# A two-layer decoder trunk on one core: where the split weights begin in their tiles, and where four rows of vectors are loaded

## The chip, the cores and the metric

The kernel runs on one core of a Trainium2 chip. The core has a matrix engine (TensorE, PE in the profile; its weight loads have a row of their own, PEld), a vector engine (VectorE, DVE), a scalar engine (ScalarE, ACT), GpSimd (POOL) and SyncE (SP), which issues most transfers. The metric is the device time of one execution in microseconds (us). Before the change it is 1217.22 us, the median of three runs (1217.1 to 1217.29).

## The reference

Two layers over 512 tokens of width 1024, float32 throughout. Layer 0 mixes with sliding-window attention and a short gated convolution, layer 1 with gated linear attention (GLA). Each is followed by a gated MLP with a width-3 causal convolution between its two projections, and by a gated per-layer embedding.

```python
def _conv_ffn(h, w_up, conv_w, conv_b, w_down):
    u = _causal_depthwise_conv(h @ w_up, conv_w) + conv_b
    gate, up = jnp.split(u, 2, axis=-1)
    return (jax.nn.gelu(gate, approximate=False) * up) @ w_down

def reference(x, p, positions, mix_norm, ffn_norm, ffn_w_up, ffn_conv_w, ...):
    cos, sin = _rope_tables(positions)
    for i in range(DEPTH):
        j = i // 2
        h = _rms_norm(x, mix_norm[i])
        if i % 2 == 0:
            x = x + _attn_conv_mixer(h, cos, sin, hy_w_in[j], ..., hy_sinks[j], hy_conv_w[j], hy_w_out[j])
        else:
            x = x + _gla_mixer(h, gla_w_in[j], gla_w_gate_up[j], ..., gla_w_out[j])
        x = x + _conv_ffn(_rms_norm(x, ffn_norm[i]), ffn_w_up[i], ffn_conv_w[i], ffn_conv_b[i], ffn_w_down[i])
        x = x + _per_layer_embedding(x, p[i], ple_norm[i], ple_w_gate[i], ple_w_proj[i])
    return x
```

The widths that matter: `D_MODEL` 1024, `D_FF` 2816 (so `w_up` is 1024 x 5632 and `w_down` 2816 x 1024), 8 query heads of 64 with blocks of 128 queries.

## The kernel before

**Products.** Features lie on the partitions and the 512 tokens along the free dimension. Every large product is made of float32 operands that are split in two: a high part, which ScalarE writes by copying to float32r, and a low part, the remainder, which VectorE writes. A product of two split operands is three matmuls into one PSUM bank, high by high, high by low and low by high. `mm3` (L153 to L159) issues them for the plain products; its rows in the profile are L157, L158 and L159. The weight is the stationary operand, 128 rows by 128 columns, and 512 tokens stream past it. In the value columns of the GLA mixer (`Values`, L1509) it is the other way round: the normed input is stationary, and 336 or 368 columns of a weight stream.

**Block products.** A part of the MLP's two projections is not done plainly. `seven` (L850) computes a two by two block of weights against a two by two block of activations with seven block products in place of eight. Its inner function `product` has four steps of three matmuls (L865, L866, L867), each of them 256 tokens wide. One call of `seven` is 7 x 4 x 3 = 84 matmuls. It is called for each of the 11 column groups of the up projection in both layers, four times in the first down projection and three times in the second, 29 calls in all. Its weights come in four tiles: `plain`, `t13` and `last` are split into the tiles `wh` and `wl` (by `cut_blocks` at L804 with `wide`, or by `first_forms` at L824), and `t2`, which serves one of the seven block products, into two smaller tiles of the pool `sp`.

**Tiles.** `wh` and `wl` are tags of the pool `wp`: three buffers each, 1024 elements of four bytes per partition, one behind the other. Ahead of them in the pool stand two buffers `raw` of 8,192 bytes, into which the weights are loaded. Each of the six tiles of 4,096 bytes begins at a multiple of 512 bytes of its partition, and every stationary block of 128 columns is 512 bytes of it. The normed inputs (tags `a0`, `a1`, `b0`, `b1`) and the forms for the block products (tag `four`) begin at multiples of 256 bytes. In `Values` a step of the weight is 336 or 368 elements, 1,344 or 1,472 bytes, so that the streamed operand of every second step begins 64 bytes behind a multiple of 128. The plain products split their weights with `cut` (L118). Behind `wp` lie the pools `sp` and `sm` and those of the stages, the last of which ends 696 bytes short of the partition's 229,376 bytes.

**Order.** TensorE runs in the order in which the kernel writes its matmuls (`manual_schedule`); on the other engines the framework's scheduler chooses. In layer 0's mixer `behind(n)` hangs work behind the n-th of 96 steps of the input projection (`conv_in`, eight contraction steps for each of 12 outputs). Behind step 88 (`probs_at[3]`) stand the mixture of block 2, the transposes of block 3's probabilities (`probs`, L625, rows L633, L639, L641) and then `load_vectors_ffn(0)`; behind step 93 (`mix_at`) stands the mixture of values for block 3 (`mix`, L643, row L650). `load_vectors_ffn` takes the MLP's convolution weights and biases in two calls of `columns` (L198): transfers from GpSimd's queue into a tile `vrow` (two buffers), one transpose on TensorE (L216), one copy by ScalarE (L217). The same function is called again for layer 1.

**Around it.** In an up projection one turn of the loop over groups is 84 matmuls of 256 columns, 48 of 512 columns for the value columns (`value`, L940), and the convolution taps on VectorE (`taps`, L913, rows L919 and L925), whose input is the tile `z` with a row of 514 elements, of which 512 are used.

Of the kernel before, what the change touches and what calls it, by code (L numbers as in the profile page):

```python
# [9 lines left out]
F32 = mybir.dt.float32  # L10
# [4 lines left out]
ALU = mybir.AluOpType  # L15
# [41 lines left out]
class Kernel:  # L57
# [51 lines left out]
    def weights(self, src, na, nb, by="b"):  # L109
        raw = self.raw(na, nb)  # L110
        self.nc.sync.dma_start(raw, src)
        return self.cut(raw, by)

    def raw(self, na, nb):
        t = self.wp.tile([P, 2048], F32, tag="raw", name=self.nm("raw"), bufs=2)
        return t[:, : na * nb].rearrange("p (a b) -> p a b", b=nb)

    def cut(self, rv, by, pool=None, bufs=3):  # L118


        nc = self.nc
        pool = pool or self.wp
        na, nb = rv.shape[1:]
        parts = []
        n = 2 if na * nb > 1024 else 1
        for k in range(n):
            if by == "b":
                a, b = na, nb // n
                v = rv[:, :, k * b : (k + 1) * b]
            else:  # L130
                a, b = na // n, nb
                v = rv[:, k * a : (k + 1) * a, :]
            h = pool.tile([P, 1024], F32R, tag="wh", name=self.nm("wh"), bufs=bufs)
            l = pool.tile([P, 1024], F32R, tag="wl", name=self.nm("wl"), bufs=bufs)
            hv = h[:, : a * b].rearrange("p (a b) -> p a b", b=b)
            lv = l[:, : a * b].rearrange("p (a b) -> p a b", b=b)
            nc.scalar.activation(hv, v, AF.Copy)  # L137
            nc.vector.tensor_tensor(lv, v, hv.bitcast(F32), ALU.subtract)  # L138
            parts.append((hv, lv))

        def get(i, c0, c1):
            if by == "b":
                b = nb // n
                k = c0 // b
                h, l = parts[k]
                return h[:, i, c0 - k * b : c1 - k * b], l[:, i, c0 - k * b : c1 - k * b]
            a = na // n
            h, l = parts[i // a]
            return h[:, i % a, c0:c1], l[:, i % a, c0:c1]

        return get
# [268 lines left out]
    def mixer0(self):  # L420
        nc, a, tc = self.nc, self.a, self.tc
        with tc.tile_pool(name="m0", bufs=1) as mp:
# [65 lines left out]
            sink = self.sm.tile([P, 16], F32, name="sink", bufs=1)[:, :NQ]  # L488
            self.late(sink[:, :1])
            nc.gpsimd.dma_start(sink, a["hy_sinks"][0:1, :].partition_broadcast(P))  # L490
            nsink = self.sm.tile([P, 16], F32, name="nsink", bufs=1)[:, :NQ]
            nc.vector.tensor_scalar_mul(nsink, sink, -1.0)
            h = HD // 2

            def normed(x, tab):
# [76 lines left out]
            def scores(t):  # L572

                w = 2 * P if t else P
                k0 = (t - 1) * P if t else 0
                mask = self.amask if t else self.amask[:, P:]
                s = ss[t] = mp.tile([P, NQ, 2 * P], F32, tag="s", name=self.nm("s"), bufs=2)
                mx, nm, den, es = (self.few(8, g) for g in ("mx", "nm", "den", "es"))
                banks = []
                for h2 in range(2):  # L580

                    pbs = [self.pa(), self.pa()]
                    banks.append(pbs)
                    for hh in range(2):
                        hq = 2 * h2 + hh
                        for g in range(2):
                            nc.tensor.matmul(
                                pbs[g][:, hh * 256 : hh * 256 + w],
                                qTs[t][64 * g : 64 * g + 64, hq, :],
                                kT[64 * g : 64 * g + 64, k0 : k0 + w],  # L590
                                start=True, stop=True,
                            )
                for h2, pbs in enumerate(banks):
                    heads = [(g, hh, 4 * g + 2 * h2 + hh) for hh in range(2) for g in range(2)]
                    for g, hh, head in heads:
                        nc.vector.tensor_tensor_reduce(
                            s[:, head, :w], pbs[g][:, hh * 256 : hh * 256 + w], mask,
                            scale=1.0, scalar=-1e30, op0=ALU.add, op1=ALU.max,
                            accum_out=mx[:, head : head + 1],
                        )  # L600

                    nc.vector.scalar_tensor_tensor(
                        out=of(nm, h2), in0=of(mx, h2), scalar=-(HD**-0.5), in1=of(nsink, h2), op0=ALU.mult,
                        op1=ALU.min,
                    )
                    nc.vector.tensor_tensor(of(es, h2), of(nm, h2), of(nsink, h2), ALU.subtract)
                    nc.scalar.activation(of(es, h2), of(es, h2), AF.Exp)
                    for g, hh, head in heads:
                        nc.scalar.activation(
                            s[:, head, :w], s[:, head, :w], AF.Exp, bias=nm[:, head : head + 1], scale=HD**-0.5,  # L610
                            accum_out=den[:, head : head + 1],
                        )
                    nc.vector.tensor_tensor(of(den, h2), of(den, h2), of(es, h2), ALU.add)
                    nc.vector.reciprocal(of(den, h2), of(den, h2))
                    h = 4 + 2 * h2
                    nc.vector.tensor_tensor(
                        s[:, h : h + 2, :w], s[:, h : h + 2, :w],
                        den[:, h : h + 2].unsqueeze(2).to_broadcast([P, 2, w]), ALU.mult,
                    )
                    for head in (2 * h2, 2 * h2 + 1):  # L620
                        nc.scalar.activation(s[:, head, :w], s[:, head, :w], AF.Copy, scale=den[:, head : head + 1])
# [122 lines left out]
                        query_turned(t + 2, qn[t + 2], self.ps)  # L744
                    probs(t)

            behind(probs_at[3])(lambda: self.load_vectors_ffn(0))
            behind(mix_at)(lambda: mix(3))
            behind(96)(lambda: conv_out(1))
            with tc.manual_schedule(engines={ET.PE}):  # L750
                R = self.spread()
# [52 lines left out]
    def cut_blocks(self, src, wide=True):  # L804

        nc = self.nc
        if wide:
            h, l = (self.wp.tile([P, 1024], F32R, tag=g, name=self.nm(g), bufs=3) for g in ("wh", "wl"))
        else:
            h, l = (self.sp.tile([P, S], F32R, tag="sq", name=self.nm("t2"), bufs=2) for _ in range(2))  # L810
        h, l = (x.rearrange("p (j n) -> p j n", n=src.shape[2]) for x in (h, l))
        nc.scalar.activation(h, src, AF.Copy)  # L812
        nc.vector.tensor_tensor(l, src, h.bitcast(F32), ALU.subtract)  # L813
        h, l = (x.rearrange("p j n -> p (j n)").rearrange("p (k n) -> p k n", n=P) for x in (h, l))
        n = 2 if wide else 1
        return lambda j, c: (h[:, n * j + c, :], l[:, n * j + c, :])
# [7 lines left out]
    def first_forms(self, ev, od, raw=None):  # L824

        nc = self.nc
        b11, b12, b21, b22 = ev[:, :, :P], ev[:, :, P:], od[:, :, :P], od[:, :, P:]
        if raw is not None:
            plain = self.cut_blocks(raw[:, :, :P])
        else:  # L830
            h, l = (self.wp.tile([P, 1024], F32R, tag=g, name=self.nm(g), bufs=3) for g in ("wh", "wl"))
            h, l = (x.rearrange("p (j u n) -> p j u n", u=2, n=P) for x in (h, l))
            for u, b in enumerate((b11, b21)):
                self.split((h[:, :, u], l[:, :, u]), b)
            plain = lambda j, c: (h[:, j, c], l[:, j, c])
        nc.vector.tensor_tensor(b11, b12, b11, ALU.subtract)
        nc.vector.tensor_tensor(b12, b22, b12, ALU.subtract)  # L837
        return plain
# [57 lines left out]
    def ffn(self, i, project, next_gain):  # L896
# [8 lines left out]
        with tc.tile_pool(name=f"ffn{i}", bufs=1) as fp:  # L905
# [5 lines left out]
                return fp.tile([P, 2, S], F32, tag="zt", name=self.nm("zt"), bufs=2)  # L911

            def taps(y, ps, f, more=None):  # L913
                z = fp.tile([P, S + 2], F32, tag="z", name=self.nm("z"), bufs=3)[:, :S]
                if more is None:
                    nc.vector.tensor_tensor(z, ps, R, ALU.mult)
                else:
# [398 lines left out]
    def ple1(self, fp):  # L1316
# [16 lines left out]

        def chunk(src):
            if count[0] % 6 < 3:
                h, l = (self.wp.tile([P, 2, H], F32R, tag=g, name=self.nm(g), bufs=3) for g in ("wh", "wl"))
            else:
                four = self.four(fp)
                h, l = four[:, :2], four[:, 2:]
            count[0] += 1  # L1340
            nc.scalar.activation(h, src, AF.Copy)
            nc.vector.tensor_tensor(l, src, h.bitcast(F32), ALU.subtract)
            return h, l
# [41 lines left out]
            return pj  # L1385

        def result():
            return fp.tile([P, S + 2], F32, tag="z", name=self.nm("so"), bufs=3)[:, :S]

        def keep(banks, tag):  # L1390
            out = []
# [33 lines left out]
        with tc.manual_schedule(engines={ET.PE, ET.DVE, ET.Activation}):  # L1425
# [30 lines left out]
            w22 = chunks(b22)  # L1456
            minus(b11, b21, b11)
            wt4 = [chunk(b11[:, :2, :])]
            nc.scalar.activation(self.few(NT, "rlo"), self.r, AF.Sigmoid)
            add(X, "s3", wt3)  # L1460
            ss = [summed(X[t], kd[t]) for t in (0, 1)]
            for t in (0, 1):
# [504 lines left out]
```

## Time and profile before

| | us |
|---|---|
| median of three runs | 1217.22 |
| the profiled execution's own time | 1216.55 |
| its span, first to last instruction | 1214.8 |
| TensorE with a matmul under way | 1207.6 |
| VectorE busy | 971.0 |
| ScalarE busy | 667.6 |
| GpSimd busy | 45.1 |

The views read are the page (busy time, the chain that ended last), the timeline (start in us, duration in us, engine, line, operation, tiles out and in, shapes, and in brackets the idle time before), the instructions of one line (durations in ns: least, median, largest) and busy time by stretches. The end of a matmul in the profile is modelled and matmuls overlap, so the pace of TensorE is read from starts: the time from one start to a later one over the number of matmuls between.

In time, the up projection of layer 0 runs from about 183 to 445 us and its down projection to 510; the same stages of layer 1 run from about 809 to 1070 and to 1117 us.

### The profile page before, as it was taken

The page shows a single profiled execution, that of the slowest core. Times are in us where ns is not written, and L with a number is a line of the kernel's source. Part 1 is how long each engine was busy: PE and PEld are TensorE (multiplying, and loading weights), DVE is VectorE, ACT ScalarE, POOL GpSimd, SP SyncE. Part 2 cuts the span into 40 slices and gives each one's busy share as a digit, 9 for nine tenths or more (in the row PEclk, how much of TensorE's full clock was granted, in tenths as well). Part 3 has the DMA queues.
Part 4 walks back from the last instruction along what each step waited for, and adds up shares of the span by engine and source line. Part 5 has one row for each costly group of instructions (what it writes and reads, how often), then busy time and mean ns, then how long its engine had stood idle before and what let it go on. Part 6 is the DMA issues. An engine that isn't in the chain of part 4 may idle for free.

```text
span 1214.8 us, 17728 instructions
## 1 busy us (share of the span) xinstructions
PE 1207.6 (99%) x7018; PEld 1049.2 (86%) x7018; DVE 971.0 (80%) x1543; ACT 667.6 (55%) x1093; POOL 45.1 (4%) x64
## 2 busy tenths in 40 slices
PE   9999999999999999999999999999999999999998
PEld 8887789999998889888988988889999999888887
DVE  6786687899998986746679876778999898978595
ACT  7466465656555644534563554555565555645374
POOL 2600000000000000000100000000000000000000
PEclk9999999999999999999999999999999999999999
DMA  7222222424242332222322222322232423322601
GB/s 220 83 93 70 73 70 76 133 70 139 70 129 79 108 120 94 95 97 85 114 93 69 73 68 70 105 83 92 81 128 70 139 70 129 123 87 96 208 1 70
DMA packets 111127, 117.61 MB, mean 97 GB/s; under 512 B 2840, under 2 KB 106322, under 8 KB 111044
## 3 DMA queue, kind: packets, MB, share of 16 engines
q1 hardware_dynamic: 109680, 115.35, 29.0%
q8 instruction: 55, 0.90, 0.3%
q0 software_dynamic: 560, 0.42, 0.3%
q10 hardware_dynamic: 804, 0.70, 0.2%
q14 instruction: 28, 0.23, 0.1%
HBM read 114.37 MB, written 2.10 MB: 96 GB/s over the span
## 4 chain that ended last, share of the span: by engine, by line
PE 92%; DVE 4%; ACT 2%; issue 0%; DMA 0%; ACTq 0%; POOL 0%; DVEq 0%
PE ps L157 13%; PE ps L158 13%; PE ps L159 13%; PE pa L158 7%; PE pa L157 7%; PE pa L159 7%; PE ps L865 6%; PE ps L867 6%; PE ps L866 6%; PE pa L867 2%; PE pa L866 2%; PE pa L865 2%; PE ps L1364 1%; PE ps L1362 1%; PE ps L1363 1%; DVE wl L138 1%
## 5 line engine op out<-in xcount | busy, mean ns | idle before, releaser
L137 ACT ACTIVATE wh<-raw 128x1024 fp32r<-128x1024 f32 (+4 forms) x154 | 152.5, 992 | 154.6 <-PE ps L158 103.2
L138 DVE TENSOR_TENSOR wl<-raw,wh 128x1024 fp32r<-128x1024 f32 (+4 forms) x154 | 175.4, 1140 | 59.2 <-ACT wh L137 58.6
L812 ACT ACTIVATE wh<-raw 128x1024 fp32r<-128x1024 f32 x78 | 82.6, 1059 | 127.8 <-DVE raw L837 65.6
L925 DVE SCALAR_TENSOR_TENSOR zt<-z,vfa,zt 128x510 f32<-128x510 f32 (+1 forms) x176 | 130.9, 746 | 11.9 <-ACT zt L923 11.2
L813 DVE TENSOR_TENSOR wl<-raw,wh 128x1024 fp32r<-128x1024 f32 x78 | 95.4, 1223 | 19.8 <-ACT wh L812 19.7
L923 ACT ACTIVATE zt<-z,vfb 128x512 f32<-128x512 f32 x88 | 71.0, 809 | 21.3 <-DVE four L976 12.8
L157 PE MATMUL ps<-b,wh 128*128 128x512 f32 x192 | 76.6, 399 | 0.0
L158 PE MATMUL ps<-b,wh 128*128 128x512 f32 x192 | 75.1, 391 | 0.0
L159 PE MATMUL ps<-b,wl 128*128 128x512 f32 x192 | 75.0, 391 | 0.0
L157 PE MATMUL pa<-a,wh 128*128 128x512 f32 x176 | 69.0, 392 | 0.0
L157 PE MATMUL pa<-b,wh 128*128 128x512 f32 x176 | 69.0, 392 | 0.0
L158 PE MATMUL pa<-a,wh 128*128 128x512 f32 x176 | 69.0, 392 | 0.0
L158 PE MATMUL pa<-b,wh 128*128 128x512 f32 x176 | 69.0, 392 | 0.0
L159 PE MATMUL pa<-a,wl 128*128 128x512 f32 x176 | 68.5, 389 | 0.0
L159 PE MATMUL pa<-b,wl 128*128 128x512 f32 x176 | 68.5, 389 | 0.0
L865 PE MATMUL ps<-four,wh 128*128 128x256 f32 x232 | 65.8, 283 | 0.0
L867 PE MATMUL ps<-four,wl 128*128 128x256 f32 x232 | 65.6, 283 | 0.0
L866 PE MATMUL ps<-four,wh 128*128 128x256 f32 x232 | 65.6, 283 | 0.0
L157 PE MATMUL ps<-a,wh 128*128 128x512 f32 x160 | 63.6, 398 | 0.0
L158 PE MATMUL ps<-a,wh 128*128 128x512 f32 x160 | 62.4, 390 | 0.0
L159 PE MATMUL ps<-a,wl 128*128 128x512 f32 x160 | 62.4, 390 | 0.0
L157 PE MATMUL ps<-uh,wh 128*128 128x512 f32 x128 | 50.3, 393 | 0.0
(472 smaller groups left out, 3517.4 us busy)
## 6 DMA issues: line engine op xcount, KB each, us to landing
raw<-in_ffn_w_up_dram SPq DMA_DIRECT2D x44, 1024.0 KB, 5.0
raw<-in_ffn_w_down_dram SPq DMA_DIRECT2D x13, 1024.0 KB, 4.7
raw<-in_hy_w_in_dram SPq DMA_DIRECT2D x8, 1024.0 KB, 5.0
raw<-in_gla_w_in_dram SPq DMA_DIRECT2D x8, 1024.0 KB, 5.1
raw<-in_ffn_w_down_dram SPq DMA_DIRECT2D x8, 768.0 KB, 4.1
raw<-in_ple_w_gate_dram SPq DMA_DIRECT2D x6, 1024.0 KB, 4.7
raw<-in_hy_w_out_dram SPq DMA_DIRECT2D x16, 256.0 KB, 4.4
raw<-in_gla_w_out_dram SPq DMA_DIRECT2D x4, 1024.0 KB, 4.7
```

Source lines behind the costliest of these rows:

```text
L137: nc.scalar.activation(hv, v, AF.Copy)
L138: nc.vector.tensor_tensor(lv, v, hv.bitcast(F32), ALU.subtract)
L157: mm(out, lh, rh, start=start, stop=False, **kw)
L158: mm(out, lh, rl, start=False, stop=False, **kw)
L159: mm(out, ll, rh, start=False, stop=stop, **kw)
L812: nc.scalar.activation(h, src, AF.Copy)
L813: nc.vector.tensor_tensor(l, src, h.bitcast(F32), ALU.subtract)
L865: mm(out, wh, xh, start=first and j == 0, stop=False, **kw)
L866: mm(out, wh, xl, start=False, stop=False, **kw)
L867: mm(out, wl, xh, start=False, stop=j == ND // 2 - 1, **kw)
L923: nc.scalar.activation(y, z, AF.Identity, scale=w2[:, f : f + 1], bias=bb[:, f : f + 1])
L925: nc.vector.scalar_tensor_tensor(out=y[:, tap:], in0=z[:, : S - tap], scalar=w[:, f : f + 1], in1=y[:, tap:], op0=ALU.mult, op1=ALU.add,)
```

## The change

The tiles `wh` and `wl` become 1056 elements long and come from one function, `weight_tiles(off)`. `cut`, and the weights of the last stage (`chunk`), take them from the tile's start; the weights of the block products (`plain`, `t13`, `last`) take 1024 elements from element 16 on, 64 bytes into the tile. The six tiles now lie 4,224 bytes apart, so they begin at 0, 128 and 256 bytes past a multiple of 512 for `wh` and at 384, 0 and 128 for `wl`; the pools behind move by 768 bytes or less. To make room, `z` and the results of the last stage lose their two spare elements, the negated sinks are written over the sinks, and the sigmoid that brings in its table writes to a tag that exists. `load_vectors_ffn(0)` is hung behind step 93, after the last mixture of values, in place of step 88. No instruction is added or removed.

```diff
--- before.py
+++ after.py
@@ -111,15 +111,20 @@
         self.nc.sync.dma_start(raw, src)
         return self.cut(raw, by)
 
+    def weight_tiles(self, off=0):
+
+        return [
+            self.wp.tile([P, 1024 + 32], F32R, tag=g, name=self.nm(g), bufs=3)[:, off : off + 1024] for g in ("wh", "wl")
+        ]
+
     def raw(self, na, nb):
         t = self.wp.tile([P, 2048], F32, tag="raw", name=self.nm("raw"), bufs=2)
         return t[:, : na * nb].rearrange("p (a b) -> p a b", b=nb)
 
-    def cut(self, rv, by, pool=None, bufs=3):
+    def cut(self, rv, by):
 
 
         nc = self.nc
-        pool = pool or self.wp
         na, nb = rv.shape[1:]
         parts = []
         n = 2 if na * nb > 1024 else 1
@@ -130,8 +135,7 @@
             else:
                 a, b = na // n, nb
                 v = rv[:, k * a : (k + 1) * a, :]
-            h = pool.tile([P, 1024], F32R, tag="wh", name=self.nm("wh"), bufs=bufs)
-            l = pool.tile([P, 1024], F32R, tag="wl", name=self.nm("wl"), bufs=bufs)
+            h, l = self.weight_tiles()
             hv = h[:, : a * b].rearrange("p (a b) -> p a b", b=b)
             lv = l[:, : a * b].rearrange("p (a b) -> p a b", b=b)
             nc.scalar.activation(hv, v, AF.Copy)
@@ -488,8 +492,7 @@
             sink = self.sm.tile([P, 16], F32, name="sink", bufs=1)[:, :NQ]
             self.late(sink[:, :1])
             nc.gpsimd.dma_start(sink, a["hy_sinks"][0:1, :].partition_broadcast(P))
-            nsink = self.sm.tile([P, 16], F32, name="nsink", bufs=1)[:, :NQ]
-            nc.vector.tensor_scalar_mul(nsink, sink, -1.0)
+            nc.vector.tensor_scalar_mul(sink, sink, -1.0)
             h = HD // 2
 
             def normed(x, tab):
@@ -600,10 +603,10 @@
                         )
 
                     nc.vector.scalar_tensor_tensor(
-                        out=of(nm, h2), in0=of(mx, h2), scalar=-(HD**-0.5), in1=of(nsink, h2), op0=ALU.mult,
+                        out=of(nm, h2), in0=of(mx, h2), scalar=-(HD**-0.5), in1=of(sink, h2), op0=ALU.mult,
                         op1=ALU.min,
                     )
-                    nc.vector.tensor_tensor(of(es, h2), of(nm, h2), of(nsink, h2), ALU.subtract)
+                    nc.vector.tensor_tensor(of(es, h2), of(nm, h2), of(sink, h2), ALU.subtract)
                     nc.scalar.activation(of(es, h2), of(es, h2), AF.Exp)
                     for g, hh, head in heads:
                         nc.scalar.activation(
@@ -744,8 +747,8 @@
                         query_turned(t + 2, qn[t + 2], self.ps)
                     probs(t)
 
-            behind(probs_at[3])(lambda: self.load_vectors_ffn(0))
             behind(mix_at)(lambda: mix(3))
+            behind(mix_at)(lambda: self.load_vectors_ffn(0))
             behind(96)(lambda: conv_out(1))
             with tc.manual_schedule(engines={ET.PE}):
                 R = self.spread()
@@ -805,7 +808,7 @@
 
         nc = self.nc
         if wide:
-            h, l = (self.wp.tile([P, 1024], F32R, tag=g, name=self.nm(g), bufs=3) for g in ("wh", "wl"))
+            h, l = self.weight_tiles(16)
         else:
             h, l = (self.sp.tile([P, S], F32R, tag="sq", name=self.nm("t2"), bufs=2) for _ in range(2))
         h, l = (x.rearrange("p (j n) -> p j n", n=src.shape[2]) for x in (h, l))
@@ -828,7 +831,7 @@
         if raw is not None:
             plain = self.cut_blocks(raw[:, :, :P])
         else:
-            h, l = (self.wp.tile([P, 1024], F32R, tag=g, name=self.nm(g), bufs=3) for g in ("wh", "wl"))
+            h, l = self.weight_tiles(16)
             h, l = (x.rearrange("p (j u n) -> p j u n", u=2, n=P) for x in (h, l))
             for u, b in enumerate((b11, b21)):
                 self.split((h[:, :, u], l[:, :, u]), b)
@@ -911,7 +914,7 @@
                 return fp.tile([P, 2, S], F32, tag="zt", name=self.nm("zt"), bufs=2)
 
             def taps(y, ps, f, more=None):
-                z = fp.tile([P, S + 2], F32, tag="z", name=self.nm("z"), bufs=3)[:, :S]
+                z = fp.tile([P, S], F32, tag="z", name=self.nm("z"), bufs=3)
                 if more is None:
                     nc.vector.tensor_tensor(z, ps, R, ALU.mult)
                 else:
@@ -1333,7 +1336,7 @@
 
         def chunk(src):
             if count[0] % 6 < 3:
-                h, l = (self.wp.tile([P, 2, H], F32R, tag=g, name=self.nm(g), bufs=3) for g in ("wh", "wl"))
+                h, l = (x.rearrange("p (a b) -> p a b", b=H) for x in self.weight_tiles())
             else:
                 four = self.four(fp)
                 h, l = four[:, :2], four[:, 2:]
@@ -1385,7 +1388,7 @@
             return pj
 
         def result():
-            return fp.tile([P, S + 2], F32, tag="z", name=self.nm("so"), bufs=3)[:, :S]
+            return fp.tile([P, S], F32, tag="z", name=self.nm("so"), bufs=3)
 
         def keep(banks, tag):
             out = []
@@ -1456,7 +1459,7 @@
             w22 = chunks(b22)
             minus(b11, b21, b11)
             wt4 = [chunk(b11[:, :2, :])]
-            nc.scalar.activation(self.few(NT, "rlo"), self.r, AF.Sigmoid)
+            nc.scalar.activation(self.few(NT, "rs", 4), self.r, AF.Sigmoid)
             add(X, "s3", wt3)
             ss = [summed(X[t], kd[t]) for t in (0, 1)]
             for t in (0, 1):
```

The order on TensorE changes in one place: the two transposes L216 stand behind the eight matmuls of the last mixture, 15 plain matmuls later than before. ScalarE's two copies L217 move with them, two splits of the mixture's result (L101) later.

## Prediction, made before the change was run

> **What bounds the kernel now.** First the page: who is busy, and whose work ends last.
>
> ```profile
> span 1214.8 us, 17728 instructions
> PE 1207.6 (99%) x7018; PEld 1049.2 (86%) x7018; DVE 971.0 (80%) x1543; ACT 667.6 (55%) x1093; POOL 45.1 (4%) x64
> PE 92%; DVE 4%; ACT 2%; issue 0%; DMA 0%; ACTq 0%; POOL 0%; DVEq 0%
> core 0: 1214.8 us, clock 1.000
> ```
>
> TensorE has a matmul under way for 99% of the span, and 92% of the chain that ended last is its own work, at the full granted clock. A change can therefore only save where it shortens the step from one matmul to the next, or one of the few waits between. So the second view is the timeline of TensorE, read from starts: a block product of 256 columns, then plain matmuls of 512.
>
> ```profile
> 183.37 0.28 PE L865 MATMUL pa<-a,wh 128*128 128x256 f32 x1
> 183.72 0.28 PE L865 MATMUL pa<-a,wh 128*128 128x256 f32 x1
> ...
> 184.80 0.40 PE L157 MATMUL pa<-a,wh 128*128 128x512 f32 x1
> ...
> 191.89 0.39 PE L157 MATMUL pa<-a,wh 128*128 128x512 f32 x1
> ...
> 192.57 0.39 PE L157 MATMUL pa<-a,wh 128*128 128x512 f32 x1
> ```
>
> From 183.72 to 184.80 lie nine matmuls of 256 columns: 0.120 us each. From 191.89 to 192.57 lie three of 512: 0.227. Twice the columns cost 0.107 more, so a column costs 0.107 / 256 = 0.417 ns, and the rest is 0.120 - 0.107 = 13.3 ns in both, the time of 32 columns. This rest, paid with each new weight, is all that an address could change. The first three from 183.37 to 183.72 took 0.35, not 0.36: one of them paid less.
>
> **The offset.** How many matmuls load a weight that now begins 64 bytes into its tile: line L865, a third of them, by weight tile.
>
> ```profile
> L865 PE MATMUL ps<-four,wh x232: 277/283/364, 193.6 to 1116.9; 128*128 128x256 f32 x116
> L865 PE MATMUL ps<-a,wh x120: 277/283/387, 187.6 to 505.6; 128*128 128x256 f32 x120
> L865 PE MATMUL pa<-four,wh x116: 277/283/287, 186.2 to 1104.1; 128*128 128x256 f32 x116
> L865 PE MATMUL ps<-b,wh x112: 277/283/387, 813.4 to 1115.5; 128*128 128x256 f32 x112
> L865 PE MATMUL ps<-four,t x88: 283/283/283, 189.1 to 1027.1; 128*128 128x256 f32 x88
> L865 PE MATMUL pa<-a,wh x60: 277/283/283, 183.4 to 497.1; 128*128 128x256 f32 x60
> L865 PE MATMUL pa<-b,wh x56: 277/283/283, 809.1 to 1106.9; 128*128 128x256 f32 x56
> ```
>
> With `wh`: 232 + 120 + 116 + 112 + 60 + 56 = 696, and as many on L866 and L867: 2088 matmuls, 2088 x 0.120 = 250.6 us of the span. The `t` rows (88 here, 28 more in smaller groups) are not touched. Each ns of step is worth 2.09 us.
>
> No row of before has a stationary weight of these products off a multiple of 128 bytes, so the cost is bounded from both sides. The nearest rows for phase are those of the GLA values, where the stream (not the weight) begins 64 bytes off in every second step of k, four token blocks, twelve matmuls, long.
>
> ```profile
> 589.56 0.33 PE L157 MATMUL ps<-wh,b 128*128 128x368 f32 x1
> ...
> 591.56 0.33 PE L157 MATMUL ps<-wh,b 128*128 128x368 f32 x1
> ...
> 593.59 0.33 PE L157 MATMUL ps<-wh,b 128*128 128x368 f32 x1
> ...
> 657.70 0.32 PE L157 MATMUL ps<-wh,b 128*128 128x336 f32 x1
> ...
> 659.53 0.32 PE L157 MATMUL ps<-wh,b 128*128 128x336 f32 x1
> ...
> 661.38 0.32 PE L157 MATMUL ps<-wh,b 128*128 128x336 f32 x1
> ```
>
> At 368 columns the aligned step takes 591.56 - 589.56 = 2.00 us (166.7 ns each), the shifted one 2.03 (169.2): 2.5 ns more. At 336 the shifted step comes first, 1.83 us (152.5 ns), the aligned one takes 1.85 (154.2): 1.7 ns less. So the phase of the two streams does count, and its sign hangs on the width. Also, 7 ns is a round size here: it is the time of 16 columns, or 64 bytes of stream (16 x 0.417 = 6.7); 2.5 ns on each of three at 368 columns is 7 ns on one of them; and it is what the first matmuls at 183.37 lacked, whose least duration is 277 ns where the median is 283. I read the rest of 13.3 ns as two such pieces, one for each half line in which the weight's stream and the tokens' stream get into each other's way, and 64 bytes as moving one against the other by one piece.
>
> Bounds: the 1.7 ns less and the 2.5 ns more of the rows above give -3.5 and +5.2 us; one piece less or more on every matmul gives 2088 x 6.67 = 13.9 us to either side. The lowest end is a pace with hardly any rest, that of the transposes, whose weights are as large:
>
> ```profile
> 125.81 1.36 PE L633 MATMUL pa<-cf,s 128*128 128x128 f32 x11
> L633 PE MATMUL pa<-cf,s x56: 272/273/327, 71.8 to 126.9; 128*128 128x128 f32 x56
> ```
>
> (1.36 - 0.27) / 10 = 0.109 us from start to start, for one weight load each; below that a product cannot go while it loads as often: (120 - 109) x 2088 = 23.0 us. I take one piece less, **-13.9 us**: the row that it comes from (277 against 283) is of the same matmuls with the same `wh`, whereas the GLA rows shift the other operand at other widths.
>
> The Trainium skill states, in "TensorE: Matmul & The Clock Gate", section Back-to-back issue gap, a warm gap of N / 2.4 + 2.5 ns, which is 109.2 ns at 256 columns; the rows here have 120. By it the 10.8 ns above it would be avoidable, 22.6 us as an estimate from that page.
>
> The matmuls of 512 columns meet the tiles too: three of the six buffers now begin 128 bytes off a multiple of 256. Stationary `wh` against streams `a` (multiples of 512 bytes) and `four` (256 past one) give the same 283 ns in the rows above, so I cost this at nothing; the bound is the same piece on a part of them, and it belongs to the slower rival.
>
> **Who keeps up.** A turn of the up projection has 84 matmuls of 256 columns and 48 of 512: 84 x 0.120 + 48 x 0.2267 = 20.96 us, of which 72 would shrink by 0.48 in all.
>
> ```profile
> 277.00:298.00 21.00, 21.00 (x134) 19.04 (x133) 20.40 (x30) 12.83 (x21) 0.00 (x0) 1.00 0.31 106
> 445.00:466.00 21.00, 21.00 (x144) 19.12 (x143) 15.63 (x23) 9.26 (x17) 0.00 (x0) 1.00 0.23 76
> L925 DVE SCALAR_TENSOR_TENSOR zt<-z,vfa,zt x176: 739/745/753, 202.5 to 1046.2; 128x511 f32<-128x511 f32 x88, 128x510 f32<-128x510 f32 x88
> ```
>
> In the fullest turns VectorE is busy 20.40 of 21.00 us (third figure of a row); a turn of about 20.5 would just hold it. If it did not, some six such turns (three a layer) would give back at most their 0.48, 2.9 us. I take 0. In the down projection VectorE has 15.63 of 21.00. That `z` loses its spare elements changes nothing there: its three buffers began at 0, 32 and 64 bytes past a multiple of 128, and all 176 taps took 739 to 753 ns. By that row I cost the splits into shifted tiles at 0 as well, and the edits of the sinks and the sigmoid's tag keep their instructions: 0.
>
> **The vectors.** The rows around the transposes that move, and around where they go:
>
> ```profile
> 126.80 0.38 PE L633 MATMUL pa<-cf,s 128*128 128x128 f32 x2
> 127.36 0.29 PE L216 MATMUL pa<-cf,vrow 88*128 88x88 f32 x1 [0.19 <-ACT pT L641]
> 127.55 0.58 ACT L641 COPY pT<-pa 128x512 f32<-128x512 f32 x1
> 127.95 1.52 POOL L207 DMA_DIRECT2D vrow<-in_ffn_conv_w_dram  x3 [51.30 <-PE pa L216]
> 128.00 0.29 PE L216 MATMUL pa<-cf,vrow 88*128 88x88 f32 x1 [0.34 <-DVE pT L639]
> 128.08 0.48 PE L157 MATMUL ps<-a,wh 128*128 128x512 f32 x1
> 128.65 0.68 DVE L639 COPY pT<-pa 128x512 f32<-128x512 f32 x1
> 131.68 1.94 PE L650 MATMUL ps<-pT,v 128*64 128x512 f32 x8
> ```
>
> Each L216 waits until a copy of the probabilities has freed a PSUM bank. The last L633 starts at 126.80 + 0.11 and is over for the issue at 127.02; the next plain matmul starts at 128.08: 1.06 us. Behind the last mixture the banks have been free for long, and two transposes cost 2 x 0.08 (128.00 to 128.08): **-0.9 us**. Late next could be the mixture L650, which comes 1.06 earlier, at 130.6; its last input is copied by 128.65 + 0.68 = 129.33, so it has 1.3 us to spare. ScalarE's two copies of the vectors (0.25 each) go behind two splits and hide in its idle time. On GpSimd's queue the transfers behind these transposes are layer 1's vectors, which waited 51.30 us for `vrow` and will wait some 4 longer, for a use hundreds of us later. If that cover were gone, the price is the 1.06 itself.
>
> **Sum.** 1216.55 (the profiled execution: span 1214.8 and 1.75 around it) - 13.9 - 0.9 = 1201.75. The median of the runs is 0.67 above this execution, so the forecast is **1202.4 us**. "The same" is within 0.2%, 2.4 us, about what a measurement of this kernel can tell from no change.
>
> **The rivals.**
> A: the rest is fixed, paid for a change of weight whatever its address. For it: 13.3 ns at 256 and at 512 columns, and at 336 about as much; against it the 2.5 ns at 368 and the 277 ns. Then only the vectors count: 1217.22 - 0.9 = 1216.3. The Trainium skill stands here, in "SBUF — State Buffer", section Who interferes with whom: TensorE has two independent read ports, one for the stream and one for weight loads, and never waits on anyone. By that page there is nothing for an offset to part.
> B: one matmul of three gains the piece, as one of three paid it at 368 columns: 2088 / 3 x 6.67 = 4.6, so 1211.7.
> C: nearly the whole rest goes, to 109 ns: -23.0, with VectorE holding the six fullest turns at 20.40 against 84 x 0.120 + 48 x 0.2267 - 72 x 0.011 = 20.17, 1.4 back: 1217.22 - 23.0 + 1.4 - 0.9 = 1194.7.
> D, the other side: a load of 512 bytes that begins in mid-line touches one half line more, so the rest grows. The place is every `wh` and `wl` of L865 to L867; the price is 2.5 ns (as at 368 columns) to 6.67 ns each, 5.2 to 13.9 us: 1221.5 to 1230.2. It decides as soon as a step is longer by 0.4 ns, which eats the 0.9 of the vectors. For it: the larger of the two phase effects seen was a loss. Against: 336 columns.
>
> **Chances.** Forecast 0.37, A 0.17, B 0.18, C 0.08, D 0.20. Faster by over 0.2%: 0.37 + 0.18 + 0.08 = 0.63; within: 0.17; slower: 0.20. The forecast's own range is 1199 (a little more than a piece) to 1206 (VectorE gives 2.9 back). For 8 in 10 it must take in A, B and C, so 1194 to 1219; D stays out.
>
> **What would show it.** Right: in the block products twelve starts of `wh` lie 1.36 us apart, not 1.44; the `t` products stay at 0.120, the plain ones at 0.227; L216 stands behind L650 without a wait, and the plain matmul follows L633 at once. Wrong: `wh` steps at 0.120 (A), three steps of 120, 120 and 113 (B), over 0.120 (D); waits of TensorE on VectorE's `wl` or banks in the up projection (the gain given back); or the 512-column steps moved.

## The result, and the profile after

| | before | after |
|---|---|---|
| median of the runs | 1217.16 us (6 runs) | 1221.80 us (6 runs) |
| profiled execution | 1216.55 us, span 1214.8 | 1221.76 us, span 1220.0 |
| ratio after / before | | 1.0041, 95% interval 1.0029 to 1.0052 |

The change made the kernel 0.4% slower, where 1.2% faster was forecast. The page of after:

```profile
span 1220.0 us, 17728 instructions
...
PE 1213.9 (100%) x7018; PEld 1045.2 (86%) x7018; DVE 970.5 (80%) x1543; ACT 666.7 (55%) x1093; POOL 45.1 (4%) x64
...
PEclk9999999999999999999999999999999999999999
...
PE 98%; DVE 2%; ACT 0%; issue 0%; DVEq 0%
```

The same 7018 matmuls, the full granted clock in every slice (the third row), VectorE as busy as before (971.0), and the chain that ended last is TensorE's even more than it was. So nothing new waits: the 5.2 us are in the steps from one matmul to the next. The view by line and tile gives least, median and greatest duration in ns. First the block products in after (their lines are now L868 to L870; the row of L865 before, 277/283/364, stands in the prediction):

```profile
L868 PE MATMUL ps<-four,wh x232: 276/278/384, 195.0 to 1120.8; 128*128 128x256 f32 x116
...
L869 PE MATMUL ps<-four,wh x232: 276/281/285, 195.2 to 1120.9; 128*128 128x256 f32 x116
...
L870 PE MATMUL ps<-four,wl x232: 276/279/284, 195.3 to 1121.0; 128*128 128x256 f32 x116
```

A duration is the step plus some 163 ns (283 against a step of 120, 389 against 226.7), so these medians stand for steps of 115 to 118 instead of 120: a gain. Now the plain products of 512 columns, before and then after:

```profile
L157 PE MATMUL pa<-a,wh x176: 389/389/396, 179.3 to 408.0; 128*128 128x512 f32 x176
...
L158 PE MATMUL pa<-a,wh x176: 389/389/398, 179.5 to 408.3; 128*128 128x512 f32 x176
...
L159 PE MATMUL pa<-a,wl x176: 388/389/393, 179.7 to 408.5; 128*128 128x512 f32 x176
```

```profile
L161 PE MATMUL pa<-a,wh x176: 387/393/401, 180.6 to 408.7; 128*128 128x512 f32 x176
...
L162 PE MATMUL pa<-a,wh x176: 390/396/398, 180.9 to 408.9; 128*128 128x512 f32 x176
...
L163 PE MATMUL pa<-a,wl x176: 390/397/401, 181.1 to 409.2; 128*128 128x512 f32 x176
```

All three medians rose, by 4, 7 and 8 ns. They had been costed at nothing. The same can be read off starts in the timeline of TensorE; first the start of twelve block products, then of the eighteen plain ones behind them, then of what follows, before and after:

```profile
283.90 0.28 PE L865 MATMUL ps<-a,wh 128*128 128x256 f32 x1
...
285.34 0.40 PE L157 MATMUL pa<-a,wh 128*128 128x512 f32 x1
...
289.44 0.28 PE L865 MATMUL pa<-a,wh 128*128 128x256 f32 x1
```

```profile
285.00 0.28 PE L868 MATMUL ps<-a,wh 128*128 128x256 f32 x1
...
286.38 0.39 PE L161 MATMUL pa<-a,wh 128*128 128x512 f32 x1
...
290.56 0.28 PE L868 MATMUL pa<-a,wh 128*128 128x256 f32 x1
```

Block products: 1.44 us before, 1.38 after (115 ns a step). Plain ones: 4.10 before, 4.18 after (232 a step). Adding up all steps of the two timelines by width, from each start on TensorE to the next, gives

- 256 columns (2691 matmuls): 331.8 us before, 325.8 after, -6.0;
- 512 columns (3419 matmuls): 788.9 before, 801.8 after, +12.9;
- all other widths together: -1.7, of which 0.6 are the steps of the vectors' own transposes and 0.4 the step from the last L633 to them.

That is the 5.2 us of the span. The vectors did what was forecast: the waits of TensorE in before had two rows for them, which after lacks, and in after's timeline the moved transposes follow the mixture at once.

```profile
PE pa L216 <- DVE pT L639: 0.3, 1, 0.3
...
PE pa L216 <- ACT pT L641: 0.2, 1, 0.2
```

```profile
131.84 1.94 PE L653 MATMUL ps<-pT,v 128*64 128x512 f32 x8
133.72 0.37 PE L220 MATMUL pa<-cf,vrow 88*128 88x88 f32 x2
133.88 0.48 PE L161 MATMUL ps<-a,wh 128*128 128x512 f32 x1
```

### The profile page after: what moved, and what is told of

It reads as the page before. It is cut to its first block, busy times and chain, and to the rows that moved or that the text cites. A ratio compares the mean times of both kernels' runs of the same rounds, so it can differ in the third digit from the quotient of the medians.

```text
span 1220.0 us, 17728 instructions
## 1 busy us (share of the span) xinstructions
PE 1213.9 (100%) x7018; PEld 1045.2 (86%) x7018; DVE 970.5 (80%) x1543; ACT 666.7 (55%) x1093; POOL 45.1 (4%) x64
## 4 chain that ended last, share of the span: by engine, by line
PE 98%; DVE 2%; ACT 0%; issue 0%; DVEq 0%
PE ps L163 15%; PE ps L162 15%; PE ps L161 15%; PE pa L162 7%; PE pa L163 7%; PE pa L161 7%; PE ps L868 6%; PE ps L869 6%; PE ps L870 6%; PE pa L869 2%; PE pa L868 2%; PE pa L870 2%; PE pa L1683 1%; PE ps L1367 1%; PE ps L1366 1%; PE ps L1365 1%
## 5 line engine op out<-in xcount | busy, mean ns | idle before, releaser
L868 PE MATMUL ps<-four,wh 128*128 128x256 f32 x232 | 65.1, 280 | 0.0
L870 PE MATMUL ps<-four,wl 128*128 128x256 f32 x232 | 64.7, 279 | 0.0
L163 PE MATMUL ps<-uh,wl 128*128 128x512 f32 x128 | 50.7, 396 | 0.0
```

Source lines behind the costliest of these rows:

```text
L163: mm(out, ll, rh, start=False, stop=stop, **kw)
L868: mm(out, wh, xh, start=first and j == 0, stop=False, **kw)
L870: mm(out, wl, xh, start=False, stop=j == ND // 2 - 1, **kw)
```

## The experiments

A product takes its matmuls in triples (`wh`, `wh`, `wl`), so the text speaks of triples: before, 360 ns at 256 columns (3 x 120) and 680 at 512 (3 x 226.7). These are the paces that a run of like products settles to. The first one or two triples of a run differ: in before, where all phases are level, a run of plain triples mostly begins with 697 and 690 and goes on at 680, and a run of block triples mostly begins with 353 and goes on at 360. "Phase" is where a tile begins in the compiled program, modulo 256 bytes. Before, all operands of these products have phase 0. After, the pitch of 4,224 bytes (16.5 x 256) gives the three `wh` tiles 0, 128, 0 and the three `wl` tiles 128, 0, 128. And the `four` tiles went from 0 to 128 as well: they lie behind the small tiles, of which the change drops two (`nsink` and the sigmoid's own), 128 bytes in all. The pitch itself moves them by six times 128 bytes more, which leaves their phase as it is.

All runs in one table. Sums of steps are of the profiled execution, worked out as above; the last column is the median less that of the kernel before on the same chip.

| kernel | phase of `wh`/`wl` | of `four` | offset in block products | 512 columns, us | 256 columns, us | median, us | against before |
|---|---|---|---|---|---|---|---|
| before | 0 | 0 | 0 | 788.9 | 331.8 | 1217.16 | |
| after | 0 and 128 | 128 | 64 | 801.8 | 325.8 | 1221.80 | +4.6 |
| e1 | 0 | 128 | 0 | 792.3 | 331.2 | 1218.37 | +1.7 |
| e4 | 0 | 128 | 0 | 792.6 | 330.9 | 1219.34 | +2.7 |
| e2 | 0 and 128 | 128 | 0 | 802.3 | 329.2 | 1225.88 | +9.2 |
| e6 | 0 | 0 | 0 | 788.8 | 331.8 | 1215.88 | -0.8 |
| e3 | 0 | 0 | 64 | 788.8 | 327.5 | 1211.36 | -5.3 |
| e8 | 0 | 0 | 64 in `wh` alone | 788.7 | 328.1 | 1211.45 | -5.2 |
| e7 | 0 | 0 | 128 | 791.1 | 332.7 | 1217.57 | +0.9 |
| e10 | 0 | 0 | 32 | 790.5 | 328.6 | 1214.18 | -2.7 |
| e9 | 0 | 0 | 192 | 787.8 | 327.1 | 1209.86 | -7.0 |
| e12 | 0 | 0 | 64 in `wh`, 192 in `wl` | 789.2 | 321.4 | 1205.98 | -10.9 |
| e5 | 0 | 0 | 64 in all products | 805.1 | 319.6 | 1218.73 | +2.0 |
| e11 | 0 | 0 | 192 in all products | 793.3 | 321.9 | 1209.46 | -7.4 |

**e1: the move and the small edits alone.** On after:

```diff
-            self.wp.tile([P, 1024 + 32], F32R, ...)
+            self.wp.tile([P, 1024], F32R, ...)
-            h, l = self.weight_tiles(16)
+            h, l = self.weight_tiles()
```

(the second edit in both block-product helpers)

> The change with the wh and wl tiles at 1,024 elements again and no offset: only the move of the vectors and the small edits are left. Theory P (the tiles' pitch of 4,224 bytes sets half of the tiles 128 bytes off a multiple of 256 and that costs the 512-column products; the offset itself gains): 1216.3 us, the 0.9 us of the vectors gained, 256-column steps 120.0 ns, 512-column steps 226.7 ns. Rival M (the move of the vectors or the small edits cost the time): 1220 us or more.

Measured: 1218.37 us, ratio 1.0014 (1.0005 to 1.0022): a loss of 1.7 between the two expectations. The 512-column steps cost 3.4 us more, which neither had: theory P had not counted `four`. Which products pay is shown by e4.

**e4: the stage tiles alone shifted.** On before, a tile of 640 bytes behind `nsink` that nothing uses:

```diff
             nsink = self.sm.tile([P, 16], F32, name="nsink", bufs=1)[:, :NQ]
+            self.sm.tile([P, 160], F32, name="pad640", bufs=1)
```

> The kernel before with 640 bytes of padding ahead of the stage pools, so that the four tiles begin 384 bytes past a multiple of 512 instead of 256, while wh, wl, a and b stay. Theory P (the phase of stationary against streamed operand modulo 256 bytes decides): products of 512 columns with four on one side and wh or wl on the other grow from 226.7 ns to between 231 and 233 ns, products of wh against a or b stay at 226.7; slower by 2 to 10 us. Rival Q (only the tile pitch within one product's hl/lh pair matters, not its phase against the other operand): 1217.2 us, no change.

Measured: 1219.34 us, ratio 1.0022 (1.0013 to 1.0030). Plain products with `four` as the streamed operand, in before and in e4:

```profile
L158 PE MATMUL ps<-four,wh x112: 389/389/398, 422.7 to 1155.0; 128*128 128x512 f32 x112
```

```profile
L158 PE MATMUL ps<-four,wh x112: 387/394/404, 423.3 to 1157.7; 128*128 128x512 f32 x112
```

TensorE's matmuls come in the same order with the same operands, and those with `four` are 5 ns longer: their triples take 696 to 704 ns, where those of `wh` with `a` or `b` stay at 680 for the most part. They make up 2.0 of the 3.7 us by which the 512-column steps grew; the rest is spread over the other products. Rival Q falls. With the vectors' 0.8 (e6) the 2.7 leave 1.9 for e1, which measured 1.7: the small edits, costed at 0 in the prediction, cost 2.7 by where they put `four`.

**e2: the pitch alone.** On after, the second edit of e1 only.

> The change with its tiles of 1,056 elements, and block products that begin at element 0 like all others. Theory P: the 512-column products stay as long as in the changed kernel (some 12.5 us over before), and the 256-column ones lose the 6 us that they had gained there, so 1228 us; they could lose more, since a 128-byte phase can reach them too. Rival O (the offset of 64 bytes is what costs, the pitch does nothing): about 1216.5 us.

Measured: 1225.88 us, ratio 1.0076 (1.0063 to 1.0089). Against e1 only the pitch is new, and it costs 9.2 - 1.7 = 7.5 us, 10 of them at 512 columns less 2 gained at 256 and 0.5 elsewhere. The plain row of e2 shows the same median as after:

```profile
L162 PE MATMUL pa<-a,wh x176: 389/396/402, 181.1 to 410.7; 128*128 128x512 f32 x176
```

Rival O falls: the offset is not what costs. Theory P's 1228 is 2.1 us too high, since the 256-column steps keep 2.6 of the 6.0 us that they had gained. From e2 to after, with the offset added, the loss shrinks from 9.2 to 4.6. So after is made up of -0.8 (vectors, e6) and +2.7 (`four`, e4), which e1 has as 1.7 in one, then +7.5 (pitch) and -4.6 (offset).

**e6: all phases 0, no offset.** On after, a pitch of 4,352 bytes (17 x 256). `nsink` and the sigmoid's tile are as they were before, which leaves `four` at 0. To make room, constants lie closer together, and `ones` is made in a temporary tile (its two later readers take `ones_r`):

```diff
-            self.wp.tile([P, 1024 + 32], F32R, ...)
+            self.wp.tile([P, 1024 + 64], F32R, ...)
-        self.ones = self.cp.tile([P, P], F32, name="ones")
+            ones = self.sp.tile([P, S], F32, tag="acc", name="ones", bufs=1)[:, :P]
-        col = self.cp.tile([P, -(-n // 64) * 64], F32, name=name)[:, :n]
+        col = self.cp.tile([P, -(-n // 16) * 16], F32, name=name)[:, :n]
-            h, l = self.weight_tiles(16)
+            h, l = self.weight_tiles()
```

> As the kernel of e3 with an offset of 0: every operand begins at a multiple of 256 bytes, as before the change. Theory P: 512-column triples 680 ns, 256-column triples 360 ns, only the vectors' 0.9 us are gained: 1215.7 to 1216.3 us. Rival: the pitch of 4,352 bytes or the other places of the tiles count by themselves, 1212 us or less, or 1218 us or more.

Measured: 1215.88 us, ratio 0.9992 (0.9983 to 1.0001), both sums as before; theory P's number. Only the vectors' 0.8 are left, and a pitch other than 4,096 costs nothing as such. The interval just takes in no change at all; the trace is clearer, where the steps of the moved transposes and the one ahead of them are 1.0 us shorter than before.

**e3: the same with the offset of 64 bytes in the block products** (`weight_tiles(16)` kept).

> The change with tiles of 1,088 elements, a pitch of 4,352 bytes that is a multiple of 256, and the offset of 64 bytes in the block products kept; room for it comes from narrower columns of constants. Theory P: 512-column steps back at 226.7 ns, wh and wl steps of the block products at 113.3 ns, so -13.9 - 0.9 us: 1202.4 us. Rival O: the offset brings nothing of its own, 1216 to 1222 us.

Measured: 1211.36 us, ratio 0.9956 (0.9944 to 0.9968). Neither expectation: the 512-column steps are back, as theory P had it, but the gain at 256 columns is 4.3 us and not 13.9. Triples take 353.3 ns, one piece of 6.67 less and not three, and the three matmuls share it: nearly all steps take 117 to 119 ns. Rows of e6, then of e3:

```profile
L869 PE MATMUL ps<-four,wh x232: 277/283/364, 192.9 to 1116.1; 128*128 128x256 f32 x116
```

```profile
L869 PE MATMUL ps<-four,wh x232: 276/281/367, 192.7 to 1111.8; 128*128 128x256 f32 x116
```

The timeline of e3 also holds two runs of products with tiles of the same names, at the same phases, at two paces (each row but the fourth is the start of a triple):

```profile
193.16 0.28 PE L869 MATMUL ps<-four,wh 128*128 128x256 f32 x1
...
193.50 0.28 PE L869 MATMUL ps<-four,wh 128*128 128x256 f32 x1
...
193.84 0.28 PE L869 MATMUL ps<-four,wh 128*128 128x256 f32 x1
...
194.18 0.40 PE L161 MATMUL pa<-a,wh 128*128 128x512 f32 x1
...
197.72 0.28 PE L869 MATMUL ps<-four,wh 128*128 128x256 f32 x1
...
198.07 0.28 PE L869 MATMUL ps<-four,wh 128*128 128x256 f32 x1
...
198.42 0.28 PE L869 MATMUL ps<-four,wh 128*128 128x256 f32 x1
...
198.78 0.28 PE L869 MATMUL ps<-a,wh 128*128 128x256 f32 x1
```

0.34 us a triple at 193, 0.353 at 198. So 340 can be had at this offset, and the pace looks like more than a matter of phases; a run keeps the pace that it fell into. All of e3's runs say when: of its 116 runs of block products, the 104 that TensorE enters without a wait take 353 ns a triple, and of the 12 that begin behind a wait (a step at least 80 ns longer than usual, as in both runs shown) nine take 340.

**e8, e7, e10, e9: other offsets in the block products**, each on e3: 64 bytes in `wh` alone, then 128, 32 and 192 bytes in both.

```diff
-  [:, off : off + 1024] for g in ("wh", "wl")
+  [:, o : o + 1024] for g, o in (("wh", off), ("wl", 0))
```

(e8; the others are `weight_tiles(32)`, `(8)` and `(48)`)

> As the kernel of e3 with the offset of 64 bytes in wh alone, wl at its tile's start, so that one triple's stationary tiles differ from each other by 64 bytes. Theory U (a step is set by its own operands, each wh or wl on its own): two of three loads still shifted, between 353 and 358 ns a triple, 1211 to 1215 us. Rival V (the step from one stationary tile to the other counts: what shortened the triples of the changed kernel to 340 ns was that wh and wl differed): under 353 ns a triple, under 1211 us.

Measured: 1211.45 us, ratio 0.9956 (0.9942 to 0.9971), 353.3 ns a triple: theory U's lower end. That `wl` is shifted too brings nothing.

> As the kernel of e3 with an offset of 128 bytes instead of 64 in the block products, so that both of their stationary tiles stand 128 bytes off the streams but not off each other. Theory P (128 bytes between stationary and streamed operand cost at 512 columns; at 256 columns the kernel of e2 had 354 to 358 ns a triple with mixed phases): 256-column triples 352 to 360 ns, 1211 to 1216 us. Rival T (what counts is only that stationary and streamed operand differ, by 64 or by 128 bytes alike): 353.3 ns a triple, 1211.4 us.

Measured: 1217.57 us, ratio 1.0007 (0.9998 to 1.0017), 360 to 361 ns a triple. Rival T falls. The time is 1.6 over theory P's range. In the profiled execution, itself 1.0 over the median, the 512-column steps rose by 2.3 us though their tiles are those of e6. Some 1.3 of that are waits in the last stage, two of which e6's list of waits lacks:

```profile
PE pa L325 <- DVE acc L283: 0.3, 1, 0.3
PE ps L1366 <- ACT a L101: 0.3, 1, 0.3
```

The other 1.0 is in the plain products that alternate with the block products: a sign, with the two paces of e3, that a product hands its pace on to the next.

> As the kernel of e3 with an offset of 32 bytes in the block products. Theory Y (pieces of 64 bytes decide; 32 bytes stay within a piece): either as offset 0, 360 ns a triple and 1215.9 us, or as offset 64, 353.3 ns and 1211.4 us. Rival: the phase counts in finer steps, 356.7 ns a triple, 1213.6 us.

Measured: 1214.18 us, ratio 0.9978 (0.9968 to 0.9988), 354 to 355 ns a triple, and 1.7 us more at 512 columns. Neither fits whole: the triples are nearest theory Y's 353.3, but single ones lie anywhere from 349 to 359 ns, and the time is nearest the rival's.

> As the kernel of e3 with an offset of 192 bytes (64 short of the next multiple of 256) in the block products. Theory W (only how far the two operands are apart modulo 128 bytes counts): 353.3 ns a triple, 1211.4 us. Rival X (the sign counts: the operand that is behind is a piece later): 340 or 366.7 ns a triple, 1206.8 or 1220.4 us.

Measured: 1209.86 us, ratio 0.9943 (0.9928 to 0.9958). 352.8 ns a triple as theory W has it; 1.5 us below its time, 1.0 of it from shorter 512-column steps.

**e5, e11: the offset in every product with `wh` or `wl`**, 64 and 192 bytes, on e3 (`weight_tiles(16)` or `(48)` in `cut` and `chunk` too).

> As the kernel of e3 (pitch 4,352 bytes), with the offset of 64 bytes in every product that uses wh or wl, the plain ones of 512 columns too. Theory R (the offset parts stationary from streamed operand and saves one 6.67 ns piece in three steps, whatever the width): about 1,000 triples of 512 columns at 673.3 instead of 680 ns, -6.7 us against e3: 1204.7 us. Rival S (at 512 columns the gain isn't there, or turns into a loss): 1211.4 us or more.

Measured: 1218.73 us, ratio 1.0017 (1.0008 to 1.0027). Theory R falls: at 512 columns the 64 bytes cost a piece on every matmul, 700 ns a triple, where at 256 they save:

```profile
L162 PE MATMUL pa<-a,wh x176: 392/396/398, 181.0 to 407.5; 128*128 128x512 f32 x176
...
L870 PE MATMUL ps<-four,wh x232: 276/276/282, 195.4 to 1117.8; 128*128 128x256 f32 x116
```

The block products have the same phases here as in e3, but four in five of their triples now take 340 ns (the same row of e3 reads 276/281/282): 7.9 us less than in e3. Only the plain products between them differ.

> As the kernel of e5 (every product that uses wh or wl is offset) with 192 bytes instead of 64. Theory W: as e5, 512-column triples 700 ns and 256-column ones 340 ns, 1218.7 us. Rival X: at 512 columns no loss (680 ns a triple), 1200 to 1212 us, or a larger one (720 ns), 1235 us.

Measured: 1209.46 us, ratio 0.9941 (0.9926 to 0.9956). 687 ns a triple at 512 columns, one piece more, not three and not none: both expectations miss, though the time lies in rival X's first range. The block products average 343 to 347. Waits act the other way round than in e3: of 102 runs entered without a wait 75 take 340 ns, of 14 behind a wait ten take 353. And the pace lasts: the run behind a wait at 940 us and the seven after it take 353, until from 982 us on the same loop's runs are back at 340.

**e12: `wh` 64 and `wl` 192 bytes off**, on e3 (`("wl", 3 * off)` in place of 0 in e8's edit).

> As the kernel of e3, but in the block products wh begins 64 and wl 192 bytes into its tile, 128 bytes apart as in the changed kernel, while the 512-column products stay at multiples of 256. Theory Z (the 340 ns triples of the changed kernel and of e5 come from the phase in which the 512-column products around them leave TensorE): no more 340 ns triples than in e3, 353.3 ns, 1211.4 us. Rival V (the 128 bytes between wh and wl made them): 340 to 348 ns a triple, 1204 to 1209 us.

Measured: 1205.98 us, ratio 0.9912 (0.9896 to 0.9929), the fastest here, 10.9 us under the kernel before. Theory Z's forecast fails and rival V's comes true: the plain products have 680 ns, as in e3, and still the block products settle at 340 (341 to 345 on average). V can't be the whole account, though: in e5 and e11 `wh` and `wl` have the same offset, and most triples take 340 all the same. The rows of e12, and twelve of them in the timeline:

```profile
L161 PE MATMUL pa<-a,wh x176: 389/389/396, 178.1 to 403.0; 128*128 128x512 f32 x176
...
L869 PE MATMUL ps<-four,wh x232: 276/276/388, 192.2 to 1105.7; 128*128 128x256 f32 x116
```

```profile
280.92 0.28 PE L869 MATMUL ps<-a,wh 128*128 128x256 f32 x1
...
282.28 0.40 PE L161 MATMUL pa<-a,wh 128*128 128x512 f32 x1
...
286.38 0.28 PE L869 MATMUL pa<-a,wh 128*128 128x256 f32 x1
```

Twelve starts in 1.36 us, what the prediction named as its sign, and eighteen plain ones in 4.10 as before. At the head of a run the pace is first taken up: there triples of 357 and 343 ns come ahead of the 340.

## Why the prediction was wrong

- **The bound** was right. TensorE's steps set the time, and all of the difference was in them.
- **The pieces** were right for a settled triple, which moved by multiples of 6.67 ns: 340, 353.3, 360 and 680, 686.7, 700. They are not pieces of one matmul (e3's three steps share one), and values between stand at the heads of runs, at a distance of 32 bytes (e10) and at the phases of 128.
- **"So I cost this at nothing"** for the matmuls of 512 columns is the step that failed. It was argued from `a` against `four`, 256 bytes apart modulo 512, that the phase doesn't count; but the pitch made distances of 128 bytes, which the rows it was argued from don't have. e2 against e1 prices it at +7.5 us. The bound beside it, a piece on a part of them, would have been about the right size (half of 3419 x 6.67 ns is 11.4 us), but no rival carried it: D spoke of the block products alone.
- **The small edits at 0** failed in the same way. They keep their instructions but save 128 bytes ahead of `four`, and that cost 2.7 us (e4). The taps on `z` took 747 ns in the median, 745 before: no cost there, as forecast.
- **The offset, -13.9 us,** had the right sign and was mis-sized. On level ground (e3 against e6) it is 4.5 us, a piece for every three matmuls. That is rival B's price, 4.6, and nearly its time (1211.36 against 1211.7), but not its mechanism: the steps are not 120, 120 and 113. In after the offset brings 4.6. A piece on nearly every matmul needs more than the 64 bytes: in e12, `wl` 128 bytes off `wh` (256-column steps 10.4 us under e6's).
- **The row that the piece was taken from** (277 against 283 ns) was misread. In before, where all phases are level, 105 of the 106 first triples of a run of block products take 350 to 357 ns (triples with a wait left out), and 572 of the 580 later ones 358 or more. The 277 marks the first matmul behind plain products, not an address. The GLA rows were misread too: modulo 256, 1,344 bytes (336 columns) are 64 and 1,472 (368 columns) are 192, so phase and width changed together, and those rows can't show that the sign hangs on the width.
- **VectorE keeping up at 0** was right: with 10.4 us saved in e12, the list of TensorE's waits there has the same four single ones as in e6. Beside them, two places of the up projections (316 and 937 us) hold TensorE 0.2 and 0.3 us longer.
- **The vectors, -0.9 us,** were right: e6 measured -0.8 (interval -2.1 to 0.1), with both waits gone and 1.0 us less in the steps there.
- **The rivals.** A (a fixed rest) falls: the step does depend on addresses. C's 109 ns was not reached; the settled steps went down to 113.3. The time landed at D's lower end by luck: D's mechanism is not what happened, since the block products became faster. The Trainium skill's section Who interferes with whom in "SBUF — State Buffer" gives TensorE two independent read ports and says that it never waits on anyone. That doesn't account for these runs, and the measurement decides: e4 changes nothing for TensorE but where the tiles of the stages, `four` among them, begin, and takes 2.7 us longer.

Open is why a distance of 64 bytes gains at 256 columns and loses at 512, why 128 between `wh` and `wl` helps the one while 128 between plain operands hurts the other, and how a product hands its pace on. The runs show the first two by their times, and that a pace is handed on by e5 against e3 and by the runs behind waits in e3 and e11; the mechanism in TensorE they don't show.

## What to carry to other kernels

When weights change with every matmul, where tiles begin is part of the schedule: list the phase of every operand of the hot products before and after an edit, also of tiles that the edit doesn't name but pushes along. Try an offset with all other phases held (a pitch that is a multiple of 256 bytes), and price each width by itself. An edit that removes a few bytes ahead of a pool is not free until the pools behind it have been looked at.

## What the runs showed of the hardware

TensorE's step for products of two 128-row operands in this form was 0.417 ns a column plus a rest, and the rest was 13.3 ns at equal phase. In settled runs a triple moved by multiples of 6.67 ns, so that the rest of a matmul went down to 6.7 ns at 256 columns (340 ns a triple, e12) and up to 20 at 512 (700, e5). It depends on the distance of the operands' addresses, with a sign (64 bytes 700, 192 bytes 687 at 512 columns), and on more than these: at equal phases e3 has runs at 340 and at 353, and e5 at 340 what e3 has at 353. What ran just before decides with it: the plain products are all that differs between e5 and e3, and within e3 the 104 runs of block products entered without a wait all take 353, nine of the 12 behind a wait 340. At other offsets a wait did the opposite (e11, where eight runs in a row stayed at 353 behind one) or nothing (e8, all 116 runs at 353). No experiment sets such a wait by itself.
